# First norm to feed-forward: a fourth up tile in the norm's PSUM banks, a hand-written order, and double banks (a, d) and (c, b)

## Chip, core and metric

The kernel runs on one core of one Trainium2 chip. The metric is the device time of that core in microseconds (us). Three timed runs of the kernel before gave 1603.46, 1598.80 and 1600.66 us; their median, 1600.66 us, is the time before.

## The reference, cut to what matters

One layer of a diffusion backbone over 1024 tokens of width 1024. Two attentions are merged, the result goes through a layer norm, and then a feed-forward with a convolution of width 3 along the tokens follows, with a second layer norm:

```python
y = _latent_token_mixer(h, kv_ctx, ...)
x = _layer_norm(DEEPNORM_ALPHA * x + gate1 * y, ln1_g, ln1_b)      # first norm
h = x * (1.0 + scale2) + shift2
u = h @ w_up                                                       # 1024 -> 2 * 2816
u = conv_width_3(u) + conv_b
gate, val = jnp.split(u, 2, axis=-1)
y = (jax.nn.silu(gate) * val) @ w_down                             # 2816 -> 1024
x = _layer_norm(DEEPNORM_ALPHA * x + gate2 * y, ln2_g, ln2_b)
```

The change lies between the first norm and the first tiles of `h @ w_up`. What is computed stays the same.

## The kernel before

**Precision.** Every matrix product is made of three matmuls (`mm3`, L87 to L90): each operand is split into a high part and the low rest (`split`, L78: a cast to the high part, then a subtraction for the low part), and high by high, high by low and low by high are summed in PSUM. A product can start its first matmul with the high parts; the low part of the weight is read by the third.

**Feed-forward tiles.** The 2816 gate channels make 22 tiles j of 128, each with its 128 value channels (gv 0 is gate, gv 1 is value). Tiles 0 to 2 (`NCL = 3`) are computed directly: a product `u{gv}_{j}` over 8 blocks of 128 input channels, 24 matmuls per 512 tokens, in a PSUM tile of two banks. Their weights come through `up_weights` (L1158), the sequence is in `up_conv` (L1275). Tiles 3 to 21 (`up_tile`, L1360) use seven block products in place of eight, each of 12 matmuls of 128x512, in four accumulators a, b, c, d of one PSUM bank each. In the order before they are A11 into a, S2 into b, S1 into c, S3 into d, A12 onto a, S4 onto c, A22 onto d. The products A11, A12 and A22 take blocks of the raw weights (`ru0_j`, `ru1_j`, loaded by `wload`, L1322); S1 to S4 take sums of blocks, made on GpSimd (`wsums`, L1330). `pairs` (L1339) splits each of these seven into high and low: the cast is on ScalarE, the low part on VectorE (A11, S2, S1, S3, A12) or GpSimd (S4, A22), by the table `UE` (L57). On the token side, S1 and S3 take the operands T1 and T3, S2 and A22 take T2 and T4; these are differences of halves of h, made by `build(k)` (L1108) for k = 0 to 3 (`t13`, `t24`, split into T13h, T13l, T24h, T24l).

**After the products.** `conv3` (L1232) is one ScalarE pass and two VectorE passes; then comes a Silu on ScalarE, and `gated` (L1242) is two VectorE operations and three DMAs on SyncE's queue. In `up_tile`, ScalarE copies a (into `pv`, later into `ug`) and c (into `uv`), and VectorE adds b and d. S4 is accumulated onto c, so it must follow the copy `uv <- c` (L1372).

**First norm.** The tokens come in three slices of 512, 256 and 256 (`LN1_S`). `ln_steps` (L1013) makes the statistics and broadcasts them through PSUM (`sml`: two single banks); `apply` (L1049) and `emit1` (L1079) then write the modulated h as `B{k}_{half}`, high and low. While a slice is being normed, TensorE works on `u0_0`, `u1_0` and `u0_1` (three PSUM tiles of two banks, `big`, L882) with the slices that are ready (L1292 to L1298). `u1_1`, `u0_2` and `u1_2` follow when conv3 has read one of these three tiles.

**What sets the order.** TensorE's order is the program's from L1173 on (a manual schedule). The other engines are ordered by the scheduler, which follows the program and the `pend` list: `build` is put there with a distance of 2400 (`BLD`), so that its steps come between the products of tiles 0 to 2. SyncE issues the DMAs in its own order. Every engine runs its queue strictly in order: one instruction that waits holds all behind it. Small SBUF buffers are handed out from a list of free 4 KB slots (`ht` and `hput`), so a tile can be made to wait until a DMA has read the slot's last holder. Raw weights rotate through three buffers (`raw`).

**PSUM.** The norm and tiles 0 to 2 use banks 0 to 5 (`big`) and 6 and 7 (`sml`). Then a new pool of eight single banks is opened; the up tiles take them in the order `PSU` (L55).

## Time and profile before

| | us |
|---|---|
| median of three runs | 1600.66 |
| the profiled execution, device time | 1605.64 |
| its span, first to last instruction | 1603.9 |
| TensorE busy in the span | 1538.9 (96%) |
| VectorE, ScalarE, GpSimd busy | 1180.8, 813.6, 730.7 |

The profiled execution lies 4.98 us above the median of the timed runs and 1.74 us above its own span. PE is TensorE's matmuls, PEld its weight loads, DVE VectorE, ACT ScalarE, POOL GpSimd, SP SyncE. In a timeline a row gives start, duration, engine, line, operation and tiles without their numbers; in brackets stands the idle time of that engine just before, and what ended it. In a table of stretches, a row gives the stretch and its length, the busy time and the number of instructions of each engine, the granted TensorE clock as a share of the full one, the DMA share and GB/s.

### The profile page before, as it was taken

How to read it: one execution, taken by the hardware profiler on the slowest of the kernel's cores; microseconds unless marked ns; L12 is line 12 of the kernel's file. 1: busy time of each engine (PE TensorE's matmuls, PEld its weight loads, DVE VectorE, ACT ScalarE, POOL GpSimd, SP SyncE). 2: the span in 40 equal slices, each digit the busy share in tenths (PEclk: the TensorE clock that was granted, in tenths of full speed). 3: DMA queues.
4: the chain of work that ended last, by engine and by line, in shares of the span. 5: the costliest groups of instructions: out<-in, count | busy, mean ns of one | idle time of the engine just before them, and what ended most of it. 6: DMA issues, size and time to landing. Idle time of an engine off the chain costs nothing.

```text
span 1603.9 us, 22190 instructions
## 1 busy us (share of the span) xinstructions
PE 1538.9 (96%) x7748; PEld 1278.2 (80%) x7748; DVE 1180.8 (74%) x1768; ACT 813.6 (51%) x1450; POOL 730.7 (46%) x727
## 2 busy tenths in 40 slices
PE   6999999999998999999999999899999999999997
PEld 5878788888877887777688987688888888888887
DVE  7797646628887777888684788588888788656884
ACT  5422222448887667688431564344544444435552
POOL 0673202426666556665422454366667665021021
PEclk9999999999999999999999999999999999999999
DMA  9695662322236565531451223233334446996831
GB/s 378 225 315 185 199 211 84 118 83 65 61 114 142 137 134 136 122 74 33 164 168 41 79 80 105 93 106 105 105 106 105 106 113 175 354 286 207 260 108 53
DMA packets 112368, 230.00 MB, mean 143 GB/s; under 512 B 12960, under 2 KB 27808, under 8 KB 112160
## 3 DMA queue, kind: packets, MB, share of 16 engines
q1 hardware_dynamic: 96816, 198.93, 37.5%
q0 software_dynamic: 10400, 20.19, 8.3%
q10 hardware_dynamic: 5040, 9.46, 1.6%
q8 instruction: 61, 1.00, 0.3%
q14 instruction: 51, 0.42, 0.1%
HBM read 177.35 MB, written 65.86 MB: 152 GB/s over the span
## 4 chain that ended last, share of the span: by engine, by line
PE 77%; DVE 10%; ACT 4%; DMA 4%; issue 4%; POOL 2%; SPq 0%; DVEq 0%; ACTq 0%; POOLq 0%
PE ptr L529 5%; PE p L88 4%; PE p L89 4%; PE p L90 4%; PE g L88 2%; PE g L89 2%; PE g L90 2%; PE s L412 2%; PE av L550 2%; PE b L90 2%; PE b L89 2%; PE c L88 2%; PE c L89 2%; PE c L90 2%; PE b L88 2%
## 5 line engine op out<-in xcount | busy, mean ns | idle before, releaser
L539 DVE TENSOR_TENSOR ptl<-ptr,pth 128x512 fp32r<-128x512 f32 x188 | 124.6, 684 | 30.0 <-ACT pth L538 27.8
L529 PE MATMUL ptr<-ident,p 128*128 128x128 f32 x816 | 127.7, 279 | 11.6 <-DVE ptl L539 6.8
L538 ACT CAST pth<-ptr 128x512 fp32r<-128x512 f32 x188 | 106.6, 588 | 58.0 <-PE ptr L529 32.8
L85 DVE TENSOR_TENSOR ld<-rd,hd 128x1024 fp32r<-128x1024 f32 x77 | 94.8, 1249 | 50.0 <-ACT hd L80 44.9
L424 ACT ACTIVATE p<-p,nm 128x1024 f32<-128x1024 f32 (+2 forms) x128 | 125.3, 981 | 11.1 <-DVE p L457 10.3
L529 PEld LDWEIGHTS ptr<-ident,p 128*128 128x128 f32 x816 | 94.5, 141 | 42.1 <-DVE ptl L539 13.6
L80 ACT CAST hd<-rd 128x1024 fp32r<-128x1024 f32 x77 | 79.4, 1050 | 81.9 <-PE p L90 55.1
L550 PE MATMUL av<-pth,VT 128*128 128x512 f32 x236 | 104.9, 445 | 1.0 <-ACT avs L556 0.5
L88 PE MATMUL p<-hd 128*128 128x512 f32 x264 | 103.2, 391 | 0.0
L89 PE MATMUL p<-ld,hd 128*128 128x512 f32 x264 | 102.8, 390 | 0.0
L90 PE MATMUL p<-hd,ld 128*128 128x512 f32 x264 | 102.8, 389 | 0.0
L90 PE MATMUL g<-hh,wlg 128*128 128x512 f32 x256 | 99.8, 390 | 0.5 <-POOL wlg L85 0.5
L88 PE MATMUL g<-hh,whg 128*128 128x512 f32 x256 | 99.9, 390 | 0.0
L89 PE MATMUL g<-hl,whg 128*128 128x512 f32 x256 | 99.6, 389 | 0.0
L551 PE MATMUL av<-ptl,VT 128*128 128x512 f32 x236 | 97.8, 415 | 1.8 <-POOL ptl L85 1.8
L85 POOL TENSOR_TENSOR wlg<-wg,whg 128x512 fp32r<-128x512 f32 x32 | 44.1, 1385 | 115.0 <-ACT whg L80 115.0
L457 DVE TENSOR_SCALAR_CACHE_REDUCE p<-s,cvt,nmc 128x1024 f32<-128x1024 f32 x64 | 84.4, 1339 | 12.7 <-PE s L413 12.0
L412 PE MATMUL s<-KL,q 128*128 128x512 f32 (+2 forms) x192 | 76.3, 397 | 2.9 <-ACT p_x L424 2.0
L186 DVE CUSTOM_DVE_ANT_0 wml<-wml,sc,bmc 128x1024 f32<-128x1024 f32 x32 | 47.0, 1478 | 42.7 <-DMA wml<-in_wmodT_dram 40.8
L413 PE MATMUL s<-KL,q 128*128 128x512 f32 (+2 forms) x192 | 71.9, 375 | 0.0
L80 ACT CAST wS<-s 128x512 fp32r<-128x512 f32 x76 | 45.8, 621 | 50.0 <-POOL s L1077 45.8
L82 POOL TENSOR_SCALAR pth<-prw 128x512 fp32r<-128x512 f32 x48 | 31.1, 649 | 87.5 <-ACT prw L535 62.2
(420 smaller groups left out, 4955.9 us busy)
## 6 DMA issues: line engine op xcount, KB each, us to landing
wml<-in_wmodT_dram SPq DMA_DIRECT2D x48, 512.0 KB
ru<-in_w_up_dram SPq DMA_DIRECT2D x38, 512.0 KB
rd<-td SPq DMA_DIRECT2D x55, 256.0 KB
rd<-sd SPq DMA_DIRECT2D x44, 256.0 KB
rd<-in_w_dn_dram SPq DMA_DIRECT2D x33, 256.0 KB
wm<-in_wmodT_dram SPq DMA_DIRECT2D x16, 512.0 KB
wg<-in_w_g_dram SPq DMA_DIRECT2D x32, 256.0 KB
sgd<-sg ACTq DMA_DIRECT2D x32, 256.0 KB
```

Source lines behind the costliest of these rows:

```text
L80: nc.scalar.copy(hi, src)
L85: lo_eng.tensor_tensor(out=lo, in0=src, in1=hi.bitcast(F32), op=ALU.subtract)
L88: nc.tensor.matmul(ps, a[0], b[0], start=start, stop=False, skip_group_check=resumed)
L89: nc.tensor.matmul(ps, a[0], b[1], start=False, stop=False, skip_group_check=resumed)
L90: nc.tensor.matmul(ps, a[1], b[0], start=False, stop=stop, skip_group_check=resumed)
L412: nc.tensor.matmul(o, self.q[0][:, hs], ks, start=True, stop=False)
L424: nc.scalar.activation(p, s, AF.Exp, bias=nm[:, h:h + 1], scale=scale, accum_out=sm[:, h:h + 1])
L529: nc.tensor.transpose(tr[:, h * P:(h + 1) * P], self.pslice(h, n), ident)
L538: nc.scalar.copy(hi, tr)
L539: nc.vector.tensor_tensor(out=lo, in0=tr, in1=hi.bitcast(F32), op=ALU.subtract)
L550: nc.tensor.matmul(self.av, v, hi, start=first, stop=False)
L551: nc.tensor.matmul(self.av, v, lo, start=False, stop=self.left == 0)
```

## The change

1. **A fourth early tile.** After the last norm slice's steps have been issued, the pool of the norm's two single banks is released, and `u1_1` gets both. Its products with the first two token slices are issued ahead of the third slice of all four tiles. Before, `u1_1` waited for a `big` tile.
2. **A hand-written order** on VectorE, ScalarE and GpSimd from there through tile 3 (`manual_schedule(engines=MAN)`). All operands T13 and T24 of k = 0 and 1 come ahead of the first convolution; k = 2 and 3 are placed between convolutions. Tile 3's weights are loaded and split between them. The convolutions of tile 2 (`conv_in(2, 0)`, `conv_in(2, 1)`, `gate_out(2)`) move into tile 3.
3. **Tile 3 in double banks.** a and d are the halves of one two-bank tile `ad`, c and b those of `cb`, which takes `u1_1`'s banks. Its products come in the order A11, S1, S3, S2, A12, S4, A22. The pool of single banks is opened after tile 3, and `PSU` is rotated: tile 3 lies in banks 0, 1, 6 and 7, tile 4 in 4, 5, 2, 3, tile 5 in 0, 1, 6, 7. Before, tile 3 lay in 6, 7, 2, 3 and tile 4 in 4, 5, 0, 1.
4. In tile 3, the weights of tile 4 are loaded after A12 has been split, its sums are made after `gate_out(2)`, and the splits of S2, S1 and S3 of tile 4 stand behind tile 3's Silu.

The core of the diff:

```diff
-BLD = 2400.0
-PSU = 6, 7, 2, 3, 4, 5, 0, 1
+PSU = 4, 5, 2, 3, 0, 1, 6, 7
...
+    ps3s = tc.alloc_tile_pool(name="ps3s", bufs=1, space=PSUM, reuse_waits="tile")
...
-    for j, gv in ((0, 0), (0, 1), (1, 0)):
+    early = (0, 0), (0, 1), (1, 0)
+    for j, gv in early:
         up_start(j, gv)
     for si, s in enumerate(LN1_S):
         drain((len(LN1_S) - 1 - si) * (KT + 3))
-        for j, gv in ((0, 0), (0, 1), (1, 0)):
+        if s.stop == T:
+            ps3s.release()
+            ps3s = tc.alloc_tile_pool(name="ps3c", bufs=1, space=PSUM, reuse_waits="tile")
+            ups[1, 1] = ps3s.tile([P, T], F32, tag="big4", name="u1_1"), upw.pop((1, 1)), set()
+            early += (1, 1),
+            up_mm(1, 1, LN1_S[:si])
+        for j, gv in early:
             up_mm(j, gv, [s])
...
-    for k in range(4):
-        pend += [(BLD, fn) for fn in build(k)]
-    for j in range(NCL):
-        up_conv(j)
...
+    with tc.manual_schedule(engines=MAN):
+        for k in (0, 1):
+            built[k][0]()
+            built[k][1]()
+        for k in (0, 1):
+            built[k][2]()
+            built[k][3]()
+        built[2][0]()
+        built[2][1]()
+        conv_in(0, 0)
+        up_weights(2, 0)
+        conv_in(0, 1)
+        up_weights(2, 1)
+        gate_out(0)
+        built[2][2]()
+        built[2][3]()
+        conv_in(1, 0)
+        built[3][0]()
+        built[3][1]()
+        wload(NCL)
+        wsums(NCL, tm)
+        built[3][2]()
+        conv_in(1, 1)
+        pairs(NCL, "A11")
+        built[3][3]()
+        pairs(NCL, "S1")
+        gate_out(1)
+        pairs(NCL, "S3", "S2")
...
     def up_tile(j):
-        a, b, c, d = (bank(f"{n}{j}") for n in "abcd")
+        first = j == NCL
+        if first:
+            ad, cb = big(f"ad{j}"), ps3s.tile([P, T], F32, tag="big4", name=f"cb{j}")
+            a, d, c, b = (t[:, h] for t in (ad, cb) for h in (lohalf, hihalf))
+        else:
+            a, b, c, d = (bank(f"{n}{j}") for n in "abcd")
...
+        if first:
+            pairs(j + 1, "A11")
         prod(j, "S4", c, False, True)
         add(ug[:, hihalf], c, ve)
         conv3(tg, ug, j)
         nc.scalar.activation(tg, tg, AF.Silu)
         pairs(j + 1, "S2", "S1", "S3")
```

**TensorE at the end of the second token slice.** In the rows, `u0_0` is the gate product of tile 0, `B0_1` the first block of h for the second half of the tokens, `hwu` and `lwu` are the weights' high and low parts. Before:

```order
L90 MATMUL u0_1_9858<-B7_1_9955,lwu0_1_9847 128x256
L88 MATMUL u0_0_9856<-B0_1_9878,hwu0_0_9698 128x256 [waits Activation_49]
L89 MATMUL u0_0_9856<-B0_1_9878,hwu0_0_9698 128x256 [waits Pool_49]
L90 MATMUL u0_0_9856<-B0_1_9878,lwu0_0_9699 128x256
L88 MATMUL u0_0_9856<-B1_1_9899,hwu0_0_9698 128x256 [waits Activation_49]
L89 MATMUL u0_0_9856<-B1_1_9899,hwu0_0_9698 128x256 [waits DVE_49]
```

And with the change:

```order
L89 MATMUL u0_1_9861<-B7_1_9958,lwu0_1_9850 128x256
L87 MATMUL u1_1_10147<-B0_0_9445,hwu1_1_9855 128x512 [waits DVE_49,PE_49]
L88 MATMUL u1_1_10147<-B0_0_9445,hwu1_1_9855 128x512
L89 MATMUL u1_1_10147<-B0_0_9445,lwu1_1_9856 128x512
L87 MATMUL u1_1_10147<-B1_0_9495,hwu1_1_9855 128x512
L88 MATMUL u1_1_10147<-B1_0_9495,hwu1_1_9855 128x512
```

Between the second slice's last product and the third slice's first now stand 48 matmuls of `u1_1`, 24 of 128x512 and 24 of 128x256; before, `u1_1` came after the third slice, as 48 of 128x512. The other three tiles' rows are as they were.

**ScalarE from tile 2's last convolution to tile 4's splits.** `T24h_3` is the high part of the last token operand, `wS2_4` the high part of tile 4's weight for product S2, `tg3` the gate side of tile 3. Before:

```order
L1233 ACTIVATE c1_2_10445<-u1_2_10382,cvt_70 128x1024 [waits PE_49]
L80 CAST wA11_4_10584<-ru0_4_10560 128x512 [waits DMAHW0_49]
L1368 COPY pv3_10507<-a3_10503 128x512 [waits PE_49]
L80 CAST wS2_4_10617<-s12_4_10564 128x512 [waits Pool_49]
L1115 CAST T24h_3_10465<-t24_3_10458 128x1024 [waits DMAHW3_49,DVE_49,Activation_49]
L80 CAST wS1_4_10620<-s12_4_10564 128x512 [waits PE_49]
L1372 COPY uv3_10509<-c3_10505 128x512 [waits PE_49]
L80 CAST wS3_4_10623<-s34_4_10565 128x512
```

And with the change, from tile 3's copy of a to tile 4's A22:

```order
L1452 COPY ug3_10516<-ad3_10513 128x512 [waits DVE_49,PE_49]
L79 CAST wA11_4_10619<-ru0_4_10540 128x512 [waits DMAHW0_49]
L1233 ACTIVATE tg3_10519<-ug3_10516,cvt_70 128x1024 [waits DMAHW4_49,DMAHW5_49,DVE_49,Activation_49]
L1458 ACTIVATE tg3_10519<-tg3_10519 128x1024 [waits DVE_49,Activation_49]
L79 CAST wS2_4_10639<-s12_4_10599 128x512 [waits Pool_49]
L79 CAST wS1_4_10642<-s12_4_10599 128x512
L79 CAST wS3_4_10645<-s34_4_10600 128x512 [waits Pool_49]
L79 CAST wA12_4_10731<-ru0_4_10540 128x512
L79 CAST wS4_4_10734<-s34_4_10600 128x512 [waits Pool_49]
L79 CAST wA22_4_10737<-ru1_4_10541 128x512 [waits DMAHW7_49,PE_49]
```

`T24h_3` no longer stands here: it is ahead of tile 3 and its row is `[waits Pool_49]` alone. The six casts of tile 4 behind A11 stood ahead of tile 3's gate convolution and now stand behind its Silu.

**SyncE, the loads of tile 5's second and tile 6's first raw weights.** Before:

```order
L1325 DMA ru1_5_10705<-in_w_up_dram 128x1024 [waits DMAHW4_49,DVE_49]
L1325 DMA ru0_6_10848<-in_w_up_dram 128x1024 [waits DMAHW7_49,DMAHW5_49,Pool_49]
L1247 DMA td3_82<-tg3_10511 128x512 [waits DMAHW6_49,DVE_49]
L1248 DMA td3_82<-tg3_10511 128x512
L1249 DMA td3_82<-tv3_10510 128x2x512 [waits DMAHW0_49,DVE_49,Activation_49]
```

And with the change:

```order
L1310 DMA ru1_5_10741<-in_w_up_dram 128x1024 [waits DMAHW7_49,DMAHW4_49,Pool_49]
L1310 DMA ru0_6_10884<-in_w_up_dram 128x1024 [waits DMAHW5_49,DVE_49]
L1247 DMA td3_82<-tg3_10519 128x512 [waits DMAHW6_49,DVE_49]
L1248 DMA td3_82<-tg3_10519 128x512
L1249 DMA td3_82<-tv3_10518 128x2x512 [waits DMAHW0_49,DVE_49,Activation_49]
```

The two loads have exchanged buffers: `ru1_5` now waits for GpSimd's low part of A22 of tile 4, the last user of `ru1_4`, where before it waited for VectorE's low part of A12 of tile 4.

More of the change, by code (lines that the diff above doesn't have):

```diff
@@ L885, in sml @@
     def sml(name, w=512):
-        return ps3.tile([P, w], F32, tag="sml", name=name, bufs=2)
+        return ps3s.tile([P, w], F32, tag="sml", name=name, bufs=2)
     def weight(src, nm, n=8, tag="w", he=None, le=None, rtag="raw"):
@@ L1295, in layer_kernel @@
         drain((len(LN1_S) - 1 - si) * (KT + 3))
-        for j, gv in ((0, 0), (0, 1), (1, 0)):
+        if s.stop == T:
[5 more added lines that the diff above has]
+        for j, gv in early:
             up_mm(j, gv, [s])
             if s.stop == T:
-                ups[j, gv][2].add(HALF)
-    cs = [hfree.pop(0) for _ in range(2)]
-    for k in range(4):
-        pend += [(BLD, fn) for fn in build(k)]
-    for j in range(NCL):
-        up_conv(j)
-    drain()
-    hput(*[f"B{k}_1" for k in range(4)])
-    ps3.release()
-    ps3 = tc.alloc_tile_pool(name="ps3u", bufs=1, space=PSUM, reuse_waits="tile")
-    ubanks = list(PSU)
-    def bank(name):
-        n = ubanks.pop(0)
-        ubanks.append(n)
-        return ps3.tile([P, HALF], F32, tag=f"u{n}", name=name)
-    for n in range(8):
-        ps3.tile([P, HALF], F32, tag=f"u{n}", name=f"u{n}")
+                ups[j, gv][2].update((0, HALF))
     def wload(j):
@@ L1346, in pairs, with conv_in, gate_out, bank @@
             split(wsrc.pop((j, n)), t[:, 0], t[:, 1], nc.scalar, getattr(nc, UE[list(prods).index(n)]))
+    cs = [hfree.pop(0) for _ in range(2)]
+    built = [build(k) for k in range(4)]
+    cv = {}
+    def conv_in(j, gv):
+        if gv == 0:
+            hslot[f"c0_{j}"] = pool, tag = cs[j % 2]
+            t = pool.tile([P, T], F32, tag=tag, name=f"c0_{j}", bufs=1)
+        else:
+            t = ht(f"c1_{j}")
+        conv3(t, ups.pop((j, gv))[0] if (j, gv) in ups else u2[gv], gv * NF + j)
+        cv[j, gv] = t
+    def gate_out(j):
+        g, v = cv.pop((j, 0)), cv.pop((j, 1))
+        nc.scalar.activation(g, g, AF.Silu)
+        gated(j, g, v)
+        hput(f"c1_{j}")
+    MAN = {mybir.EngineType.DVE, mybir.EngineType.Activation, mybir.EngineType.Pool}
+    with tc.manual_schedule(engines=MAN):
[26 more added lines that the diff above has]
+        pairs(NCL, "S3", "S2")
+    for gv in (0, 1):
+        up_mm(2, gv, [hsl(0), hsl(1)])
+    u2 = [ups.pop((2, gv))[0] for gv in (0, 1)]
+    drain()
+    hput(*[f"B{k}_1" for k in range(4)])
+    hfree[:] = hfree[-4:] + hfree[:-4]
+    ubanks = list(PSU)
+    def bank(name):
+        n = ubanks.pop(0)
+        ubanks.append(n)
+        return ps3.tile([P, HALF], F32, tag=f"u{n}", name=name)
     def prod(j, n, o, start, stop):
@@ L1360, in up_tile @@
     def up_tile(j):
-        a, b, c, d = (bank(f"{n}{j}") for n in "abcd")
+        first = j == NCL
+        if first:
+            ad, cb = big(f"ad{j}"), ps3s.tile([P, T], F32, tag="big4", name=f"cb{j}")
+            a, d, c, b = (t[:, h] for t in (ad, cb) for h in (lohalf, hihalf))
+        else:
+            a, b, c, d = (bank(f"{n}{j}") for n in "abcd")
         pv = ht(f"pv{j}", (P, 2, HALF))
@@ L1368, in up_tile @@
         nc.scalar.copy(pe, a)
-        prod(j, "S2", b, True, True)
-        add(ve, b, pe)
+        if first:
+            conv_in(2, 0)
+            pairs(j, "A12")
+            wload(j + 1)
+        else:
+            prod(j, "S2", b, True, True)
+            add(ve, b, pe)
         prod(j, "S1", c, True, True)
         nc.scalar.copy(uv[:, hihalf], c)
-        pairs(j, "A12", "S4", "A22")
-        if j + 1 < NF:
-            wload(j + 1)
-            wsums(j + 1, tm)
-        prod(j, "S3", d, True, True)
-        add(uv[:, hihalf], d, uv[:, hihalf])
+        if first:
+            prod(j, "S3", d, True, True)
+            add(uv[:, hihalf], d, uv[:, hihalf])
+            pairs(j, "S4")
+            conv_in(2, 1)
+            prod(j, "S2", b, True, True)
+            add(ve, b, pe)
+            pairs(j, "A22")
+            gate_out(2)
+            wsums(j + 1, tm)
+        else:
+            pairs(j, "A12", "S4", "A22")
+            if j + 1 < NF:
+                wload(j + 1)
+                wsums(j + 1, tm)
+            prod(j, "S3", d, True, True)
+            add(uv[:, hihalf], d, uv[:, hihalf])
         add(uv[:, hihalf], uv[:, hihalf], ve, nc.gpsimd)
-        pairs(j + 1, "A11")
+        if not first:
+            pairs(j + 1, "A11")
         prod(j, "A12", a, False, True)
         nc.scalar.copy(ug[:, lohalf], a)
+        if first:
+            pairs(j + 1, "A11")
         prod(j, "S4", c, False, True)
@@ L1392, in up_tile @@
         hput(*[f"{n}{j}" for n in ("pv", "ug", "uv", "tv")])
-    wload(NCL)
-    wsums(NCL, tm)
-    pairs(NCL, "A11", "S2", "S1", "S3")
-    for j in range(NCL, NF):
+    with tc.manual_schedule(engines=MAN):
+        up_tile(NCL)
+    ps3s.release()
+    ps3.release()
+    ps3 = tc.alloc_tile_pool(name="ps3u", bufs=1, space=PSUM, reuse_waits="tile")
+    for n in range(8):
+        ps3.tile([P, HALF], F32, tag=f"u{n}", name=f"u{n}")
+    for j in range(NCL + 1, NF):
         if j == NF - 1:
```

## The prediction

> **What bounds the kernel now.** I read the page first, for the engine that fills the span.

> ```profile
> span 1603.9 us, 22190 instructions
> PE 1538.9 (96%) x7748; PEld 1278.2 (80%) x7748; DVE 1180.8 (74%) x1768; ACT 813.6 (51%) x1450; POOL 730.7 (46%) x727
> ```

> TensorE (PE) is busy in 96% of the span, so time can only be won where PE stands still or runs at a lower clock. I then went through PE's timeline between the first norm and the up tiles and looked for idle time in brackets; VectorE's rows (DVE) for the last use of the norm's banks and the last operand of the third slice are added.

> ```profile
> 940.76 0.28 PE L88 MATMUL u<-B,hwu 128*128 128x256 f32 x1
> 950.48 0.28 PE L88 MATMUL u<-B,hwu 128*128 128x256 f32 x1
> 953.64 0.38 PE L89 MATMUL u<-B,hwu 128*128 128x256 f32 x1 [2.88 <-DVE B L1077]
> 963.25 0.47 PE L88 MATMUL u<-B,hwu 128*128 128x512 f32 x1 [0.43 <-DVE c L1236]
> 1007.89 0.79 PE L88 MATMUL b<-T24h,wS 128*128 128x512 f32 x1 [6.99 <-ACT T24h L1115]
> 1009.15 0.80 PE L89 MATMUL b<-T24l,wS 128*128 128x512 f32 x1 [0.47 <-DVE T24l L1077]
> ...
> 946.98 0.74 DVE L1051 TENSOR_TENSOR z<-z,bca 128x256 f32<-128x256 f32 x2
> 952.64 2.38 DVE L1077 TENSOR_TENSOR B<-v,B 128x256 fp32r<-128x256 f32 x2
> ```

> PE waits 2.88 us in the third slice for low parts of h, 0.43 for a `big` tile, and in tile 3 6.99 and 0.47 for the last token operand T24. Next the table of stretches, cut at the steps of the granted clock (length, PE busy with its count, clock, DMA share, GB/s):

> ```profile
> 791.00:794.40 3.40, 1.64 (x7) 1.00 0.65 188
> 794.40:797.80 3.40, 3.36 (x8) 0.50 0.31 125
> ...
> 951.40:954.80 3.40, 1.16 (x9) 1.00 0.10 34
> 954.80:958.20 3.40, 3.40 (x18) 0.50 0.02 5
> ...
> 999.20:1002.60 3.40, 1.70 (x8) 1.00 0.51 152
> 1002.60:1006.00 3.40, 0.00 (x0) 1.00 0.80 291
> 1006.00:1009.40 3.40, 1.05 (x2) 0.50 0.06 20
> 1009.40:1012.80 3.40, 3.40 (x9) 0.50 0.00 0
> ```

> [...]

> Last, the chain of waits tells what T24 waited for:

> ```profile
> 1003.48 3.22 DMA td<-c
> 1006.79 1.05 ACT T24h L1115
> 1007.87 1.24 DVE T24l L1077
> ```

> It is a buffer: `T24h_3` has the slot of tile 2's value side, which a DMA must first have stored.

> **The change: what goes.** PE's speed comes from two rows: from 940.76 to 950.48 lie 81 matmuls of 128x256, 0.12 us each; and one tile (84 matmuls) separates these two:

> ```profile
> 1022.55 0.69 DVE L1356 TENSOR_TENSOR ug<-c,pv 128x512 f32<-128x512 f32 x1 [4.09 <-PE c L90]
> 1041.59 0.69 DVE L1356 TENSOR_TENSOR ug<-c,pv 128x512 f32<-128x512 f32 x1 [2.86 <-PE c L90]
> ```

> 19.04 us, so 2.72 per product and 0.2267 per matmul of 128x512. The second slice ends 72 matmuls after 940.76, at 949.4. There `u1_1` now starts, since DVE's last read of the norm's bank ended at 947.7. It runs 24 x 0.2267 + 24 x 0.12 = 8.3 us, to 957.7, and the third slice's last low parts are ready at 955.0, so the first wait is gone. The third slice of four tiles takes 96 x 0.12 = 11.5, to 969.2; `u0_2` and `u1_2` take 96 x 0.2267 = 21.8, to 991.0; six products of tile 3, to the end of S4, 16.3, to 1007.3. Before, S4 ended at about 1022.45. The difference, 15.1, agrees with the 14.9 of the sum; I use 14.9.

> Nothing may wait on the way. The tightest point is the low part of `u0_2`'s weight on DVE: its buffer comes free when PE has done `u0_1` (957.7 + 72 x 0.12 = 966.4).

> ```profile
> 960.00:980.00 20.00, 19.57 (x98) 16.55 (x97) 19.73 (x21) 9.92 (x10) 4.76 (x3) 1.00 0.30 106
> 980.00:1000.00 20.00, 20.00 (x90) 16.57 (x89) 13.18 (x12) 8.95 (x12) 13.71 (x10) 1.00 0.23 79
> ```

> At 1.24 us, as `T24l` above, a subtraction of the same size, it ends at 967.6, 1.6 ahead of need. Queued behind it on DVE are the convolution of `u1_0`, `u1_2`'s low part (needed at 980.1), T13 and T24 of k = 2 and 3, two more convolutions and tile 3's splits. DVE's whole work from 960 to 1000 was 19.73 + 13.18 = 32.9 us (third busy column); without a hole it ends at 993. S2, the first to need T24, starts at 991.0 + 3 x 2.72 = 999.2. POOL has 4.76 + 13.71 = 18.5 us of work there, and SyncE's order differs only in the two exchanged loads. So these edits cost nothing under PE's 21.8 us of tile 2, with 6 us to spare; were DVE slowed by more, S2 would wait for the rest, us for us. `T24h_3` waits for no DMA any more, and S2 comes last of the first four, so k = 3 is not late. The new banks cost nothing: tiles 3 and 4 share none.

> **What is late next.** In tile 3 the splits of tile 4 stand behind the Silu on ScalarE (ACT), and S4's end starts the chain to that Silu. Its rows in tile 3 before:

> ```profile
> 1023.32 1.25 ACT L1233 ACTIVATE tg<-ug,cvt 128x1024 f32<-128x1024 f32 x1 [0.15 <-DVE ug L1356]
> 1024.61 1.28 DVE L1234 SCALAR_TENSOR_TENSOR tg<-ug,cvt,tg 128x1023 f32<-128x1023 f32 x1 [1.37 <-ACT tg L1233]
> 1025.82 0.68 DVE L1356 TENSOR_TENSOR uv<-d,pv 128x512 f32<-128x512 f32 x1
> 1026.42 1.71 DVE L1236 SCALAR_TENSOR_TENSOR tg<-ug,cvt,tg 128x1023 f32<-128x1023 f32 x1
> 1028.22 1.06 ACT L1386 ACTIVATE tg<-tg 128x1024 f32<-128x1024 f32 x1 [0.39 <-DVE tg L1236]
> 1029.65 0.62 ACT L80 CAST wS<-s 128x512 fp32r<-128x512 f32 x1
> ```

> From the add at 1022.55 to the Silu's end at 1029.28 are 6.7 us. The add of d (0.6 to the next start) now comes later, and the second DVE pass should take 1.28 in place of 1.71, as the first did: 5.7, and with 0.1 to the add, the Silu ends 5.8 after S4's end. The cast of S2 ends at 6.4. PE has A22 and tile 4's A11 until then, 5.44. Tile 4's S2 waits 1.0 us (0.6 to 1.5).

> The second wait is longer. The other casts S1, S3, A12 and S4 follow, then on GpSimd (POOL) the low parts of S4 and A22; only then is `ru1_5` loaded, three sums follow on POOL, and ACT casts S2 and S1 of tile 5. Behind these in ACT's queue stands the copy `uv <- c` of tile 4, which S4 of tile 4 needs.

> ```profile
> 1027.01 2.28 POOL L85 TENSOR_TENSOR wA<-ru,wA 128x512 fp32r<-128x512 f32 x1
> 1038.79 0.33 SPq L1325 DMA_DIRECT2D ru<-in_w_up_dram  x1
> 1042.46 1.29 POOL L1077 TENSOR_TENSOR s<-ru 128x512 f32<-128x512 f32 x1 [1.12 <-DMA ru<-in_w_up_dram]
> 1043.71 2.38 POOL L1077 TENSOR_TENSOR s<-ru,ru 128x512 f32<-128x512 f32 x1
> 1046.05 2.28 POOL L1077 TENSOR_TENSOR s<-s,ru 128x512 f32<-128x512 f32 x1
> ```

> Five casts from 5.8 at 0.62 end at 8.9; S4's low part 1.29, as a sum alone; A22's 2.28 (DVE runs beside it); the load 3.67 (1038.79 to 1042.46); sums 3 x 1.29, since DVE has nothing left then: 20.0. Two casts and the copy, 1.8: 21.8 after S4's end. PE is there after six products and the first wait, 16.3 + 1.0 = 17.3. The wait is 4.5; with casts overlapping by 0.1 each and A22's low part at 1.29 it is 2.9; with the sums at 1.29, 2.38 and 2.28 it is 6.6. I take 4.0, nearer the low end, for the idle DVE. A wait of 4.0 leaves more than 1.7 idle in at least one stretch of 3.4, so 1.7 for the clock, 3.4 if two stretches fall under the mark.

> The sum is 14.9 - 1.0 - 4.0 - 1.7 = 8.2 us won. The profiled execution would go from 1605.64 to 1597.4; the median of the runs, 4.98 lower, from 1600.66 to 1592.5.

> **The rivals.**

> *No new wait* (12%): the casts of tile 4 and the load come early enough and the full 14.9 is won, 1585.8. For it: PE has seven products between. Against it: each step of the chain is queued behind the one before, and even the shortest sum is 2.9 late.

> *Both waits at their long end* (19%): POOL and DVE slow each other throughout, as at 1043.71. Then 1.5 + 6.6 + 3.4 = 11.5 are lost, 3.4 won, 1597.3.

> *The lateness recurs, and the kernel is slower* (5%): if POOL stayed behind, each of the 17 tiles 5 to 21 would wait for its loads. At 8.2 / 17 = 0.48 us per tile nothing is won, at 0.76 it is over 4.8 slower; with 1.0 us, 1592.5 + 17 = 1609.5. For it: the exchanged buffers. Against it: POOL has time to catch up, here over two tiles (last busy column, 26.48 of 40):

> ```profile
> 1060.00:1100.00 40.00, 40.00 (x178) 33.14 (x177) 33.94 (x31) 19.54 (x28) 26.48 (x15) 1.00 0.34 110
> ```

> *The fourth tile doesn't fill the first wait* (4%): if its banks came free late, the 2.88 and their clock, and the 0.43, would stay, 5.0 in all: 1597.5. DVE's row at 946.98 speaks against it by 1.7 us.

> **How the numbers follow.** The forecast has 60%, 1592.5. The range goes from the first rival to just over the second, 1585.5 to 1598.0; outside are the recurring wait and the noise at the edges. A run-to-run difference of 0.3%, 4.8 us, is about what a measurement here can tell from none. Faster by more: nearly all of the forecast, the first rival and a third of the second, 0.76. Within: the rest of the second, the fourth, some of the forecast, 0.18. Slower: 0.06.

> **What would show it.** In the profile after, no idle time of PE in the third slice and a full clock there; ScalarE's `T24h` waiting for no DMA; S4 of tile 3 ending at about 1007; one wait of about 1 us at tile 4's S2 for a cast, and one of about 4 us at tile 4's S4 for the copy `uv <- c`, whose own wait is for POOL's sums, with one stretch at half clock behind it. I am wrong if these two are missing, if PE waits before 1007, or if tiles 5 and later wait.

## The result and the profile after

The kernel after takes 1592.85 us (median of 7 runs, 1591.08 to 1597.83), beside 1602.36 for the kernel before (7 runs, 1598.80 to 1604.43). The ratio is 0.9950 with a 95% interval of 0.9933 to 0.9967, so 5.3 to 10.7 us are won. The prediction was 1592.5.

First the page of the profiled execution (device time 1591.08), its span and engines.

```profile
span 1589.2 us, 22247 instructions
PE 1533.1 (96%) x7772; PEld 1273.3 (80%) x7772; DVE 1197.0 (75%) x1768; ACT 812.4 (51%) x1450; POOL 744.0 (47%) x727
```

Between the two profiled executions lie 14.7 us of span, and not all of this is the change. The first matmul of the second token slice starts at 940.76 before and at 931.78 after, 8.98 earlier, though the change begins only later. Part of it is three stretches at half clock (of 3.41 us each, from 180, 497 and 794 us) that the execution of before had and that of after has not. In the profiles of this study (14 kernels) that start lies anywhere from 931.78 to 940.76, and a kernel below whose instructions are the same as before's up to there (the slot alone) has it at 934.76. So I compare what the change can reach: the **stretch** from that matmul to VectorE's add of c in tile 6. It is 138.91 us before and 132.55 after. The two rows of VectorE's timeline that end it, of before and of after:

```profile
1079.67 0.69 DVE L1356 TENSOR_TENSOR ug<-c,pv 128x512 f32<-128x512 f32 x1 [1.18 <-PE c L90]
```

```profile
1064.32 0.69 DVE L1404 TENSOR_TENSOR ug<-c,pv 128x512 f32<-128x512 f32 x1 [0.86 <-PE c L89]
```

In after, the helpers of the matmuls and splits stand one line higher in the file: before's L88 to L90 and L80 are L87 to L89 and L79 here. TensorE's timeline after, with the start of the second slice, the first matmuls of six products of tile 4, and the only two waits of TensorE between the third slice and tile 6:

```profile
931.78 0.28 PE L87 MATMUL u<-B,hwu 128*128 128x256 f32 x1
...
1001.10 0.39 PE L87 MATMUL a<-B,wA 128*128 128x512 f32 x1
...
1006.38 0.50 PE L87 MATMUL b<-T24h,wS 128*128 128x512 f32 x1 [2.40 <-ACT wS L79]
...
1009.51 0.39 PE L87 MATMUL c<-T13h,wS 128*128 128x512 f32 x1
...
1014.95 0.39 PE L87 MATMUL a<-B,wA 128*128 128x512 f32 x1
...
1021.56 0.50 PE L87 MATMUL c<-B,wS 128*128 128x512 f32 x1 [3.73 <-ACT uv L1430]
...
1026.02 0.40 PE L87 MATMUL d<-T24h,wA 128*128 128x512 f32 x1
```

The waits of 2.88, 0.43, 6.99 and 0.47 are gone. In their place are 2.40 at tile 4's S2 and 3.73 at its S4, the two places that the prediction named. The row of the product behind a wait gives its full price: two products take 5.44, but from 1001.10 to 1009.51 are 8.41, so the first wait costs 2.97. The 0.57 beyond its idle time I call the refill. From 1014.95 to 1026.02 are 11.07, so the second costs 5.63 with the clock. The table of stretches of after (length, PE busy with its count, clock, DMA share, GB/s) shows which of them the clock follows:

```profile
931.80:960.30 28.50, 28.50 (x218) 1.00 0.13 41
960.30:1001.10 40.80, 40.80 (x182) 1.00 0.35 127
1002.12:1005.53 3.41, 1.86 (x9) 1.00 0.00 0
1005.53:1008.94 3.41, 2.56 (x10) 1.00 0.00 0
1019.19:1022.60 3.41, 1.04 (x4) 1.00 0.20 75
1022.60:1026.00 3.40, 3.40 (x9) 0.50 0.09 20
```

TensorE is busy without a break from the second slice to tile 4. The first wait falls into two stretches, 1.86 and 2.56 busy, and leaves the clock alone; the second leaves 1.04 in one stretch, and the next runs at half.

### The profile page after: what moved, and what is told of

It is laid out like the page before. It is cut to its first block, busy times and chain, and to the rows that moved or that the text cites. A ratio compares the mean times of both kernels' runs of the same rounds, so it can differ in the third digit from the quotient of the medians.

```text
span 1589.2 us, 22247 instructions
## 1 busy us (share of the span) xinstructions
PE 1533.1 (96%) x7772; PEld 1273.3 (80%) x7772; DVE 1197.0 (75%) x1768; ACT 812.4 (51%) x1450; POOL 744.0 (47%) x727
## 4 chain that ended last, share of the span: by engine, by line
PE 77%; DVE 10%; ACT 4%; DMA 4%; issue 3%; POOL 2%; SPq 0%; ACTq 0%; DVEq 0%; POOLq 0%
PE ptr L528 5%; PE p L88 3%; PE p L89 3%; PE p L87 3%; PE b L89 3%; PE b L88 3%; PE b L87 3%; PE g L87 2%; PE g L88 2%; PE g L89 2%; PE s L411 2%; PE av L549 2%; PE av L550 2%; PE s L412 2%; PE c L87 2%
## 5 line engine op out<-in xcount | busy, mean ns | idle before, releaser
L79 ACT CAST hd<-rd 128x1024 fp32r<-128x1024 f32 x77 | 79.4, 1050 | 82.6 <-PE p L89 52.2
L88 PE MATMUL p<-ld,hd 128*128 128x512 f32 x264 | 102.9, 390 | 0.6 <-DVE ld L84 0.6
L87 PE MATMUL p<-hd 128*128 128x512 f32 x264 | 103.3, 391 | 0.0
L89 PE MATMUL p<-hd,ld 128*128 128x512 f32 x264 | 102.8, 389 | 0.0
L87 PE MATMUL g<-hh,whg 128*128 128x512 f32 x256 | 99.9, 390 | 0.0
L89 PE MATMUL g<-hh,wlg 128*128 128x512 f32 x256 | 99.8, 390 | 0.0
L88 PE MATMUL g<-hl,whg 128*128 128x512 f32 x256 | 99.6, 389 | 0.0
L79 ACT CAST wS<-s 128x512 fp32r<-128x512 f32 x76 | 45.2, 620 | 49.6 <-POOL s L1077 48.8
```

Of the source, the lines that this page charges most:

```text
L79: nc.scalar.copy(hi, src)
L87: nc.tensor.matmul(ps, a[0], b[0], start=start, stop=False, skip_group_check=resumed)
L88: nc.tensor.matmul(ps, a[0], b[1], start=False, stop=False, skip_group_check=resumed)
L89: nc.tensor.matmul(ps, a[1], b[0], start=False, stop=stop, skip_group_check=resumed)
```

## Experiments

Each kernel was profiled once; those with an interval were also timed against the kernel before. The profile tells what happens in the stretch, since TensorE's pace there repeats to some hundredths of a us (from tile 5's add of c to tile 6's 19.03 or 19.04 us in 13 of the 14); the times of the whole kernel stand beside it. But one profile shows one position of the clock's stretches only. A wait of 2.40 at the same product was followed by full clock in after and by a stretch of 3.41 us at half in no fill, which costs 1.7 us, so a difference of that size between two kernels can be chance.

| kernel | stretch | idle time of TensorE in it | stretches at half clock in it | time, median (runs) | ratio to before, 95% |
|---|---|---|---|---|---|
| before | 138.91 | 2.88, 0.43, 6.99, 0.47 | 3 | 1602.36 (7) | |
| after | 132.55 | 2.40, 3.73 | 1 | 1592.85 (7) | 0.9950 (0.9933 to 0.9967) |
| slot alone | 128.90 | 2.88, 0.44 | 1 | 1591.05 (6) | 0.9939 (0.9920 to 0.9958) |
| no fill | 134.64 | 1.74, 2.40, 2.60 | 2 | 1596.40 (10) | 0.9973 (0.9960 to 0.9986) |
| no hand order | 132.57 | 4.87, 1.04 | 2 | 1594.25 (6) | 0.9953 (0.9935 to 0.9971) |
| tile 3 scheduled | 133.17 | 2.00, 3.84 | 2 | 1597.27 (1) | |
| add on VectorE | 132.51 | 1.49, 3.71 | 2 | 1592.19 (1) | |
| A22 ahead | 129.73 | 2.40, 1.35, 0.89 | 0 | 1591.59 (1) | |
| splits ahead | 128.59 | 1.01, 0.54, 2.10 | 0 | 1590.61 (6) | 0.9936 (0.9917 to 0.9956) |
| three splits | 129.97 | 1.61, 2.08 | 1 | 1590.25 (5) | 0.9927 (0.9913 to 0.9940) |
| three splits, add | 129.59 | 1.31, 2.15 | 1 | 1590.12 (5) | 0.9935 (0.9923 to 0.9948) |
| four moves | 130.33 | 1.15, 3.12 | 1 | 1592.21 (5) | 0.9946 (0.9930 to 0.9962) |
| four moves, less VectorE | 128.24 | 2.40 | 1 | 1588.52 (1) | |
| after, less VectorE | 132.21 | 2.40, 3.37 | 1 | 1590.94 (1) | |

Without its two waits, 2.97 and 5.63, the stretch of after would be 132.55 - 8.6 = 123.95 us: TensorE's bare work.

My theory after the result: the change removes all the old waits, worth some 15, and brings two new ones in tile 4, each with a chain of its own over the Silu, worth 8.6. The rival: most of the gain can be had without the new banks and the hand-written order.

### The slot alone

The edit goes on the kernel before, and only changes which free slot `T24h_3` gets.

```diff
         nc.scalar.activation(cv[0], cv[0], AF.Silu)
         gated(j, *cv)
-        hput(f"c1_{j}")
+        if j < NCL - 1:
+            hput(f"c1_{j}")
...
-    hput(*[f"B{k}_1" for k in range(4)])
+    hput(*[f"B{k}_1" for k in range(4)], f"c1_{NCL - 1}")
```

> The kernel before, but the value side of tile 2 gives its slot back only after the last operand T24 has got its own. Stretch: from the first matmul of the second token slice to VectorE's add of c in tile 6, 138.9 us before and 132.55 after. Theory A (the wait for the slot alone is worth 10): the waits of 6.99 and 0.47 and the two stretches at half clock go, the first wait stays; stretch 128.5 to 129.0, so shorter than with the whole change, time about 10 us under before. Theory B (taking the wait away only brings the next one, as the change did in tile 4): stretch 132 to 136.

Measured: 128.90. TensorE's larger wait that is left, ScalarE's last cast of a T24 operand, and the start of S2 in tile 3:

```profile
947.64 0.38 PE L89 MATMUL u<-B,hwu 128*128 128x256 f32 x1 [2.88 <-DVE B L1077]
...
984.40 1.05 ACT L1115 CAST T24h<-t 128x1024 fp32r<-128x1024 f32 x1 [3.04 <-DMA td<-c]
...
992.74 0.39 PE L88 MATMUL b<-T24h,wS 128*128 128x512 f32 x1
```

Theory A holds. The cast still waits for a DMA, but for one that stores tile 1, and it ends at 985.45, 7.3 ahead of S2; no later wait comes. The change of one slot wins 10.0 us of the stretch; the whole change wins 6.4. The times don't separate the two: their ratios, 0.9939 and 0.9950, have intervals that overlap. The rival is right about tile 3.

### No fill

```diff
-            up_mm(1, 1, LN1_S[:si])
         for j, gv in early:
-            up_mm(j, gv, [s])
+            up_mm(j, gv, [s] if (j, gv) != (1, 1) else list(LN1_S))
```

> The kernel after, but the first two token slices of u1_1 are computed behind the third slice of the other tiles; nothing moves on the other engines. Theory A (u1_1 covers the wait for the low parts of h): the wait of 2.9 in the third slice is back with its 1.7 of half clock, and all that follows is as much later; stretch 132.55 + 4.6 = 137.2. Theory B (the new order of the other engines had already covered it): no wait in the third slice, 132.5.

Measured: 134.64, between the two. TensorE's three waits, with VectorE's last low part of h in the third slice, and the stretches around the second wait:

```profile
948.86 0.39 PE L88 MATMUL u<-B,hwu 128*128 128x256 f32 x1 [1.74 <-DVE B L1077]
949.87 0.41 DVE L1077 TENSOR_TENSOR B<-v,B 128x256 fp32r<-128x256 f32 x1
...
1013.76 0.79 PE L87 MATMUL b<-T24h,wS 128*128 128x512 f32 x1 [2.40 <-ACT wS L79]
...
1028.97 0.50 PE L87 MATMUL c<-B,wS 128*128 128x512 f32 x1 [2.60 <-ACT uv L1429]
```

```profile
1010.00:1013.41 3.41, 1.36 (x7) 1.00 0.00 0
1013.41:1016.82 3.41, 3.06 (x7) 0.50 0.00 0
```

The wait in the third slice is back, but with 1.74 in place of 2.88, and without half clock. The hand-written order had already done part of the work: the last low part of h ends 13.2 us after the start of the second slice (950.28 - 937.12), and 14.3 before (955.02 - 940.76); without the hand order, in the next kernel, it ends at 14.3 again. So the fourth tile is worth 2.1 us of the stretch here, not the 5.0 that I gave it, and this depends on where the clock's stretches fall. The wait of 2.40 at tile 4's S2 is the same as in after, yet now it lies within one stretch and leaves 1.36 busy, and the next is at 0.50. Of these 1.7 us, 1.13 are given back, for PE comes later to S4, whose wait is 2.60 in place of 3.73.

### No hand order, and tile 3 scheduled

In the first kernel both blocks of hand-written order are left to the scheduler, in the second only that of tile 3.

```diff
-    with tc.manual_schedule(engines=MAN):
+    if True:
         for k in (0, 1):
...
-    with tc.manual_schedule(engines=MAN):
+    if True:
         up_tile(NCL)
```

> The kernel after, with the same steps in the program, but VectorE, ScalarE and GpSimd ordered by the scheduler throughout. Theory A (the hand order buys the start of u0_2 and pays in tile 4): TensorE waits some 4 us at u0_2 for its weights, with 1.7 of half clock, and not at all in tile 4 (8.6 us after); stretch 132.55 - 8.6 + 5.7 = 129.7. Theory B (the hand order is what wins): the waits of tile 3 come back, stretch 138 or more.

> The kernel after, but only the stretch up to tile 3 keeps the hand-written order; in tile 3 the scheduler orders VectorE, ScalarE and GpSimd. Theory A (the two waits of tile 4 come from the hand order of tile 3): both go, 8.6; the scheduler may bring a wait of up to 3.5 with its half clock inside tile 3; stretch 124.0 to 129.0. Theory B (the lateness is in the amount of work before tile 4): the waits of tile 4 stay, stretch 131 to 134.

Measured: 132.57 and 133.17. TensorE's larger wait in the first and both in the second:

```profile
973.86 0.76 PE L87 MATMUL u<-B,hwu 128*128 128x512 f32 x1 [4.87 <-DVE c L1236]
```

```profile
996.03 0.50 PE L87 MATMUL ad<-T13h,wS 128*128 128x512 f32 x1 [2.00 <-ACT pv L1421]
1005.62 0.80 PE L87 MATMUL ad<-B,wA 128*128 128x512 f32 x1 [3.84 <-DVE uv L1404]
```

Theory A has the place right both times, and the size too small; the second stretch lies in theory B's range. Without the hand order no wait is in tile 4, but `u0_2` waits. The larger wait is not for its weights, as I had expected, but for a convolution's last pass, which reads the PSUM tile that `u0_2` is to take; 1.04 more are for the low part of the weight. Two stretches run at half clock. (That the fourth tile had made PE early for tile 2 is argued, not shown.) With the hand order in the first part alone, the waits are in tile 3, and both are for the other half of the two-bank tile `ad`: S3 onto d begins when ScalarE has copied a, and A12 onto a when VectorE has added d. So the double banks can cost time too; no kernel here leaves them out alone. Each order has its 8.6 to 9.2 us over TensorE's bare work in another place. So the hand-written order as it stands wins nothing over the scheduler's (132.55 and 132.57; ratios 0.9950 and 0.9953).

### The addition on VectorE

```diff
-        add(uv[:, hihalf], uv[:, hihalf], ve, nc.gpsimd)
+        if not first:
+            add(uv[:, hihalf], uv[:, hihalf], ve, nc.gpsimd)
...
         nc.scalar.activation(tg, tg, AF.Silu)
+        if first:
+            add(uv[:, hihalf], uv[:, hihalf], ve)
```

> The kernel after, but in tile 3 GpSimd's addition uv <- uv + pv is made by VectorE, behind the two passes of the gate convolution; nothing else moves. Theory A (GpSimd beside it slows VectorE's second pass): that pass falls from 2.20 us to about 1.3, the Silu ends 0.9 earlier, the first wait falls from 2.40 to about 1.5, the second stays near 3.7, stretch 132.55 - 0.9 = 131.6. Theory B (the pass is slow by itself here): it stays at 2.2 and the first wait at 2.4 or a little more.

The chain to the first wait in after, on VectorE, GpSimd and ScalarE:

```profile
997.19 1.77 DVE L84 TENSOR_TENSOR wA<-ru,wA 128x512 fp32r<-128x512 f32 x1
998.88 0.68 DVE L1404 TENSOR_TENSOR ug<-cb,pv 128x512 f32<-128x512 f32 x1
1000.92 1.52 DVE L1234 SCALAR_TENSOR_TENSOR tg<-ug,cvt,tg 128x1023 f32<-128x1023 f32 x1 [1.37 <-ACT tg L1233]
1002.48 2.20 DVE L1236 SCALAR_TENSOR_TENSOR tg<-ug,cvt,tg 128x1023 f32<-128x1023 f32 x1
...
1000.06 1.30 POOL L1077 TENSOR_TENSOR s<-ru,s 128x512 f32<-128x512 f32 x1
1001.31 2.29 POOL L1404 TENSOR_TENSOR uv<-uv,pv 128x512 f32<-128x512 f32 x1
...
1004.77 1.06 ACT L1458 ACTIVATE tg<-tg 128x1024 f32<-128x1024 f32 x1 [3.88 <-DVE tg L1236]
1005.73 1.65 ACT L79 CAST wS<-s 128x512 fp32r<-128x512 f32 x3
```

And the second pass on VectorE with the addition moved behind it, and the stretches at that kernel's second wait:

```profile
1004.39 1.28 DVE L1236 SCALAR_TENSOR_TENSOR tg<-ug,cvt,tg 128x1023 f32<-128x1023 f32 x1
```

```profile
1017.65:1021.06 3.41, 1.20 (x6) 1.00 0.82 308
1021.06:1024.47 3.41, 1.91 (x5) 0.50 0.01 2
```

The second pass goes from 2.20 to 1.28, and the first wait from 2.40 to 1.49: GpSimd's addition beside it was the cause, with 0.92 us lost in a pass of 1.28. The stretch is 132.51 all the same: the second wait, 3.71 as expected, now falls across two stretches of the clock, 1.20 and 1.91 busy, both followed by half, and that takes back what was won.

### A22 ahead

```diff
         if first:
-            pairs(j + 1, "A11")
+            pairs(j + 1, "A11", "A22")
```

> The kernel after, but block A22 of tile 4 is split together with A11, ahead of S4 of tile 3, so that its raw buffer comes free some 6 us earlier; S2, S1 and S3 stay behind the Silu. Theory A (the second wait hangs on the load of ru1_5, which waits for that buffer): the first wait stays at 2.4 to 2.9, the wait at tile 4's S4 goes with its half clock, 5.6 in all; VectorE's add of d may then be late for A22 by up to 2.7, as it was with the splits ahead; stretch 127.0 to 129.6. Theory B (the second wait hangs on the Silu too): the wait at S4 stays over 2 us, stretch 131 or more.

The chain to the second wait in after: GpSimd's low parts of S4 and A22, SyncE's issue of `ru1_5`, the first of GpSimd's sums, ScalarE's two casts and the copy:

```profile
1008.49 1.29 POOL L84 TENSOR_TENSOR wS<-s,wS 128x512 fp32r<-128x512 f32 x1 [4.90 <-ACT wS L79]
1009.74 1.74 POOL L84 TENSOR_TENSOR wA<-ru,wA 128x512 fp32r<-128x512 f32 x1
1011.51 0.81 SPq L1310 DMA_DIRECT2D ru<-in_w_up_dram  x2
1015.17 1.79 POOL L1077 TENSOR_TENSOR s<-ru 128x512 f32<-128x512 f32 x1 [3.68 <-DMA ru<-in_w_up_dram]
...
1019.89 1.14 ACT L79 CAST wS<-s 128x512 fp32r<-128x512 f32 x2 [8.81 <-POOL s L1077]
1020.93 0.58 ACT L1430 COPY uv<-c 128x512 f32<-128x512 f32 x1
```

With A22 ahead, the issue and TensorE's waits behind the first:

```profile
1009.94 3.99 SPq L1310 DMA_DIRECT2D ru<-in_w_up_dram  x2
...
1023.75 0.50 PE L89 MATMUL c<-B,wS 128*128 128x512 f32 x1 [1.35 <-POOL wS L84]
...
1027.21 0.50 PE L87 MATMUL d<-T24h,wA 128*128 128x512 f32 x1 [0.89 <-DVE uv L1404]
```

Measured: 129.73. The load is issued 74.1 us after the start of the second slice, in place of 79.7. The copy is in time, the first wait is 2.40 as before, and no stretch is at half clock. A new wait of 1.35 has another cause: S4's own low part, now behind the sums on GpSimd. So the second wait does hang on the load, as theory A has it, and the stretch is just above its range.

### Splits ahead, three splits, and the addition

```diff
         add(ug[:, hihalf], c, ve)
+        if first:
+            pairs(j + 1, "S2", "S1")
         conv3(tg, ug, j)
         nc.scalar.activation(tg, tg, AF.Silu)
-        pairs(j + 1, "S2", "S1", "S3")
+        pairs(j + 1, *(("S3",) if first else ("S2", "S1", "S3")))
```

> The kernel after, but tile 3 splits S2 and S1 of tile 4 ahead of its gate convolution. ScalarE has 2.7 us idle there. Theory A (both waits of tile 4 hang on casts that queue behind the Silu): both go, 2.96 and 5.63 us with the pipeline's refill and the clock; what is late next is at most 1.5 us; stretch 124.0 to 125.5. Theory B (the second wait has its own chain, from GpSimd's low parts and the load): only the first goes, the second grows by what PE is earlier; stretch 130.5 to 132.5.

Measured: 128.59. VectorE's low part of A12 with tile 3's add of c behind it, and TensorE's waits at S3 (the first of two) and at A22:

```profile
1004.96 1.76 DVE L84 TENSOR_TENSOR wA<-ru,wA 128x512 fp32r<-128x512 f32 x1 [1.18 <-ACT wA L79]
1006.65 0.68 DVE L1404 TENSOR_TENSOR ug<-cb,pv 128x512 f32<-128x512 f32 x1
...
1015.26 0.50 PE L87 MATMUL d<-T13h,wS 128*128 128x512 f32 x1 [1.01 <-ACT wS L79]
...
1026.78 0.50 PE L87 MATMUL d<-T24h,wA 128*128 128x512 f32 x1 [2.10 <-DVE uv L1404]
```

Both waits go, as theory A has it, since the scheduler puts the casts of A12 and A22 into the same gap of ScalarE. But what is late next costs 4.6, not 1.5: S3's cast is still behind the Silu, and VectorE's add of d is late for A22. Two further kernels move S3's split between convolution and Silu, and then the addition to VectorE as well (the edit is shown against splits ahead; all that concerns `uv` is in the second kernel only):

```diff
         conv3(tg, ug, j)
+        if first:
+            pairs(j + 1, "S3")
         nc.scalar.activation(tg, tg, AF.Silu)
-        pairs(j + 1, *(("S3",) if first else ("S2", "S1", "S3")))
+        if not first:
+            pairs(j + 1, "S2", "S1", "S3")
...
-        add(uv[:, hihalf], uv[:, hihalf], ve, nc.gpsimd)
+        if not first:
+            add(uv[:, hihalf], uv[:, hihalf], ve, nc.gpsimd)
...
         prod(j, "A22", d, False, True)
+        if first:
+            add(uv[:, hihalf], uv[:, hihalf], ve)
         add(uv[:, lohalf], d, ve)
```

> As with the splits ahead, and S3 of tile 4 is split between the gate convolution and the Silu. Theory A (the waits of 1.01 and 0.54 at S3 came from its cast behind the Silu): they go, 2.1 us with the refill; VectorE's queue is 1.7 us earlier, so the wait at A22 grows by 0.4 only; stretch 128.6 - 1.7 = 126.9. Theory B (VectorE's whole queue is the limit): the wait at A22 grows by all that is won, stretch 128.6.

> As with the three splits, and in tile 3 GpSimd's addition uv <- uv + pv goes to VectorE ahead of its add of d. Theory A (GpSimd's work slows VectorE's more than the addition costs it): VectorE's queue gains 0.9 in the second pass and 0.6 at the splits and pays 0.7, the wait at A22 is 0.8 shorter; stretch 126.1. Theory B: VectorE only has more to do, stretch 127.6.

Measured: 129.97 and 129.59. Both contain a stretch at half clock, 1.7, that splits ahead didn't have; without it they would be 128.3 and 127.9. A wait at S3 stays (1.61, now for the low part on VectorE), that at A22 too (2.08). With the addition moved, S3 is free, but A12 waits 1.31 for the copy of a, and A22 2.15. Neither theory has it: the waits change places, and their sum stays near 3.5.

### Four moves, and VectorE with less to do

To the kernel of three splits and addition, the splits of A22 and of A12 are added with fixed places.

```diff
-            pairs(j + 1, "A11")
+            pairs(j + 1, "A11", "A22")
...
         nc.scalar.activation(tg, tg, AF.Silu)
+        if first:
+            pairs(j + 1, "A12")
```

> As with the three splits and the addition on VectorE, and the splits of A22 and A12 of tile 4 get fixed places too: A22 with A11, A12 behind the Silu of tile 3. With the splits ahead, the low part of A12 had slipped ahead of tile 3's add of c on VectorE and made it 2.95 us later (70.05 in place of 67.10 after the start of the second slice). Theory A (the waits left at A22 came from those 3 us): the add is back at 67.1, no wait of TensorE in tile 4 is over 0.5, stretch 124.0 to 125.0. Theory B (VectorE has too much to do in tile 4 whatever the order): the wait at A22 stays near 2, stretch 126.5 to 128.5.

Measured: 130.33. The add of c is back at 67.10, as in theory A, yet the wait at A22 is 3.12, with 1.7 of half clock behind it: theory B, above its range by that clock. VectorE's busy time is the third in this row of the table of stretches, and with TensorE's waits it says why:

```profile
1001.00:1026.00 25.00, 20.75 (x91) 16.53 (x89) 23.55 (x22) 11.98 (x19) 16.55 (x10) 1.00 0.33 115
```

```profile
1017.17 0.50 PE L87 MATMUL a<-B,wA 128*128 128x512 f32 x1 [1.15 <-ACT pv L1421]
1026.03 0.79 PE L87 MATMUL d<-T24h,wA 128*128 128x512 f32 x1 [3.12 <-DVE uv L1404]
```

VectorE is busy for 23.55 of 25 us. To test that this is what binds, the last two kernels leave out three operations of VectorE on the value side of tile 3, one on four moves, one on after.

```diff
     def conv3(t, u, c):
         nc.scalar.activation(t, u, AF.Identity, bias=cvb[:, c:c + 1], scale=cvw[:, c, 1:2])
+        if c == NF + NCL:
+            return
...
-            nc.vector.tensor_tensor(out=tv[:, 0:HALF], in0=lo, in1=hi, op=ALU.add)
+            if j != NCL:
+                nc.vector.tensor_tensor(out=tv[:, 0:HALF], in0=lo, in1=hi, op=ALU.add)
```

> As with the four moves, but VectorE leaves out three operations on the value side of tile 3 (both passes of its convolution and the sum behind the gate product: 2.00 + 1.28 + 0.69 = 3.97 us there), so that tile's result is not computed in full. Theory A (in tile 4 VectorE's amount of work is the bound: its rows stand without a hole from 1001 to 1026): the add of d comes some 4 us earlier, the wait at A22 (3.12) goes with its half clock, stretch 130.3 - 5.3 = 125.0 or down to 124.0. Theory B (the add of d is held by the splits of tile 5 ahead of it, which wait for casts and sums): the wait at A22 stays over 2, stretch 129 or more.

> The kernel after, with the same three operations of VectorE on the value side of tile 3 left out. Theory A (its two waits come from the chains over the Silu, the casts and the load, and not from VectorE's amount of work): both waits stay, 2.40 and 3.73, stretch 132.5. Theory B (VectorE's amount of work is the bound here too): the second wait falls by 2 us or more, stretch 130.5 or less.

Measured: 128.24 and 132.21. TensorE's only wait in the first:

```profile
1016.71 0.50 PE L87 MATMUL a<-B,wA 128*128 128x512 f32 x1 [2.40 <-ACT pv L1424]
```

In four moves the wait at A22 goes completely, so VectorE's amount of work held it. Part of that work may again be slowness beside GpSimd: in four moves the second pass of the gate convolution took 2.19, from 1008.50, beside a low part on GpSimd (2.27 from 1007.34), and the product of gate and value 2.20, from 1020.04, beside another (1.40 from 1019.76), where this kernel has them at 1.28 and 1.22. No run separates the two. The gain is 2.1 and not 5.3, since the wait for the copy of a has grown from 1.15 to 2.40: on ScalarE the copy stands behind the pass that reads VectorE's add of d of tile 3, and this starts 80.3 us after the start of the second slice here, 1.2 later than in four moves. In after the two waits stay (2.40 and 3.37): they come from the chains, not from VectorE's amount of work.

## Why the prediction was right, and which step of it failed

The time came out at the forecast, the mechanism is the forecast one, and no rival took place. By its terms, in the stretch:

| term | predicted | measured |
|---|---|---|
| old waits that go, with refill and clock | 14.9 | 15.3 |
| narrower matmuls of `u1_1` | 0 | -0.3 |
| tile 4's S2 | -1.0 | -3.0 |
| tile 4's S4 and its clock | -5.7 | -5.6 |
| sum | 8.2 | 6.4 |

**What goes: right.** Before, S4 of tile 4 ends 100.6 us after the start of the second slice, of which 144 x 0.12 + 300 x 0.2267 = 85.3 is work. So 15.3 were lost. (My sum had counted some 0.2 twice: the wait of 0.47 lies within the 4.9 us that I took as work at half clock.) I had put S4 of tile 3 at 1007.3 in before's time; it ends 66.6 after the start of the second slice, at 1007.4. But the fourth tile does less of it than I said (2.1 of 5.0, no fill): part of the first wait went because the hand-written order makes the low parts of h 1.1 us earlier, which I had not looked at. And the second half of `u1_1`'s tokens is now 48 matmuls of 128x256, where 24 of 128x512 stood: 5.8 in place of 5.4, the 0.3 that I had missed.

**Covers: right.** TensorE is busy without a hole from 931.80 to 1001.10, so `u0_2`'s weight, T24, the new banks and tile 2's convolutions are all in time. ScalarE's last cast of T24, which before ended a wait at 1006.79, waits for nothing and is done 17 us ahead of S2:

```profile
972.32 1.06 ACT L1115 CAST T24h<-t 128x1024 fp32r<-128x1024 f32 x1
```

**Tile 4's S2: the step that failed.** I had let VectorE's second pass take 1.28 because the add of d no longer stood between the passes. The mistake was to look only at VectorE's queue, and not at GpSimd's beside it. The passes took 1.52 and 2.20 in place of 1.28 each, beside a sum and the addition `uv <- uv + pv`, 1.16 more, and the add of c began 0.3 late behind the low part of A11: 1.46, against the 1.40 by which the wait is longer. The addition on VectorE shows 0.92 of it; the rest is read from the rows. The refill, 0.57, I had not priced. The rows that I had quoted had a pass of 1.71, from 1026.42, and I took it as due to the add between, though GpSimd's row that I quoted further down, 2.28 from 1027.01, lies beside it.

**Tile 4's S4: right.** 3.73 where I had 4.0, with the chain that I had written down: low parts, load (3.68 where I had 3.67), sums, casts, copy. A22 ahead cuts it at the load. The copy ends 1.2 us later than I had it, counted from tile 3's S4 (23.0 for 21.8), and PE is there 2.0 later (19.3 for 17.3) through the longer wait at S2, so the difference is hardly touched.

**Clock: right in its place and size,** 1.7 behind the second wait and none behind the first. That none came behind the first is luck: I had priced that wait at 1.0, and one of 2.40 at the same place cost clock in no fill.

**The time.** The stretch accounts for 6.4 of the 9.5 us between the medians. The rest is within the interval (5.3 to 10.7), and the other medians of before in this study, 1600.45, 1601.11 and 1601.79, are lower than the 1602.36 of this comparison. That the median met the forecast to 0.4 us is therefore chance in part; the trace alone would have given some 1594.

**The rival that I had not listed** is in the experiments: a change of one slot wins more of the stretch (10.0) than the change (6.4). In the order before, none of the chains binds at tile 4: its S2 is cast ahead of tile 3's Silu (at 993.43 and 1012.22 with the slot alone), and PE comes there later, 74.3 us after the start of the second slice for 69.3 in after. Which of the two decides, no run separates. With the hand-written order mended (splits ahead), the stretch is 128.59, 4.0 shorter than after's and as short as with the slot alone. By the times, three splits has the lowest ratio, 0.9927 (0.9913 to 0.9940), beside 0.9950 (0.9933 to 0.9967) of after; the intervals overlap. None of the full kernels gets near the 124 us of TensorE's bare work: where the chains over the Silu are cut, waits on VectorE take their place. Whether an order exists that has neither stays open.

## What to carry to other kernels

Before reordering an engine's work by hand, look for the one resource behind the longest wait: here one buffer's slot, worth more of the stretch than the whole change. When a wait is taken away, follow the chain to the next two and price each instruction beside what the other engines run at that moment, above all VectorE beside GpSimd (here one pass took 2.20 us beside GpSimd's addition and 1.28 without it). And compare kernels over the stretch that the change can reach: two profiled executions of the same instructions differed by 6 us before it began.

## What the runs showed of the hardware

The same wait of 2.40 us of TensorE cost clock in one kernel and none in another. In no fill it lay within one stretch of 3.41 us and left 1.36 busy, and the next was at 0.50; in after it was shared by two, with 1.86 and 2.56, and the clock stayed at 1.00. From the second slice to tile 6, the marks of the prediction held in before, in after and in eight further kernels (slot alone to A22 ahead in the table, three splits and four moves): from full clock, the most that TensorE was busy in a stretch with half clock behind it is 1.50 us (no fill, from 1027.06), and the least in one with full clock behind it 1.72 (before, from 999.18). By these rows a change that only shifts the work in time can win or lose 1.7 us, half of 3.41, per long wait. In before and after, until TensorE's work ends, every piece at half clock is 3.41 us long, but for one of 6.83 (before, from 1006.01). The four pieces at full clock between those of before are 314.03, 293.55, 157.01 and 47.79 us long, 92, 86, 46 and 14 times 3.41. Against the second slice the steps lie elsewhere in each kernel: after its start, one comes at 14.05 us in before (954.81), at 90.81 in after (1022.59) and at 76.29 in no fill (1013.41), 22.5 and 18.2 stretches later than in before.

Outside the change the marks are not exact. In before, full clock came after 1.59 busy (from 98.06) and half clock after 1.67 (from 790.97). A stretch in the first norm, busy for 3.24, was followed by full clock in before (from 876.30) and in after (from 865.58), and by half clock in no fill:

```profile
870.05:873.46 3.41, 3.24 (x23) 1.00 0.00 0
873.46:876.87 3.41, 3.41 (x10) 0.50 0.00 0
```

In before, 15 of the 22 matmuls in that stretch make a single column (128x1). So the busy time of the profile alone does not tell the next clock; what does, no run here shows.

After a stretch that was itself at half clock the marks of the prediction do not hold: a further stretch at half came after 1.91 busy in the addition on VectorE (row above) and after 2.60 in tile 3 scheduled (from 1004.81), and full clock came after 3.06 in no fill.
